# Contiguous 8 MB blocks and 64-byte result rows in a kernel that streams its input

## The chip, the cores and the metric

One core of one Trainium2 chip runs the kernel. The metric is the time of one execution on the device in microseconds (us). Ratios are the mean time of one kernel's runs over the mean of the kernel before's runs in the same rounds, so they are not quite the ratio of the medians that are quoted. Below 1 is faster than before.

Names used below: SP, ACT and DVE are the sync, scalar and vector engines. SP and ACT also issue DMAs; each has its own DMA queue (q1 for SP, q10 for ACT in the profile), and both queues are served by the same 16 DMA engines. SPq and ACTq are the instruction queues of SP and ACT. A packet is one record in the profile's list of DMA transfers: here one row of a load or store, moved by one engine. A DMA has landed when its completion semaphore says so. The pitch is the distance in memory between the starts of two neighbouring partitions' runs.

## The reference

```python
def setup_inputs():
    batch, seq, dim = 32, 512, 1024
    return {"x": np.random.randn(batch, seq, dim).astype(np.float32)}

def reference(x):
    return np.sum(np.maximum(x, 0), axis=-1).astype(np.float32)
```

That is 16384 rows of 1024 floats, 67.1 MB in and 64 KB out. Every input byte is read once.

## The kernel before

Each of the 128 partitions owns 128 consecutive rows (512 KB). A load takes 16 of a partition's rows, 64 KB in one run of addresses, so one load moves 8 MB in 128 runs that lie 512 KB apart. Seven such blocks are followed by smaller tiles of 8, 4, 2 and 1 rows, and the last row comes in four pieces, so that little work is left after the last byte. ACT sums the even rows of a tile and DVE the odd ones.

```python
xv = x_flat.rearrange("(p m) d -> p (m d)", p=P)                     # pitch 512 KB
out2d = out.rearrange("b s -> (b s)").rearrange("(p m) -> p m", p=P) # 504-byte rows in the store
big, tail, pieces = 16, [8, 4, 2, 1], [244, 252, 260, 268]
...
io_pool = ctx.enter_context(tc.tile_pool(name="io", bufs=2))
res = res_pool.tile([P, NT], fp32)
...
for j, cpd in enumerate(chunks):
    if cpd >= 8:   # the blocks and the 8-row tile share two buffers
        xt = io_pool.tile([P, cpd, D], fp32, tag="io", name=f"xt{j}")
    ...
    nc.sync.dma_start(out=xt, in_=xv[:, m0 * D : (m0 + cpd) * D]...)
    for c in range(cpd):
        m = m0 + c
        if m == NT - 2:
            act_op(xt[:, c, :], xt[:, c, :], m)
            nc.scalar.dma_start(out=out2d[:, 0 : NT - 2], in_=res[:, 0 : NT - 2])
        ...        # even rows act_op, odd rows dve_op
    m0 += cpd
...
for i, w in enumerate(pieces):       # the last row, in four pieces p0 .. p3
    ...
    nc.sync.dma_start(out=pt[:, 0:w], in_=xv[:, base + col : base + col + w])
    col += w
...                                  # DVE sums p0, p1, p2, then p3 with their sums
nc.sync.dma_start(out=out2d[:, NT - 2 : NT], in_=res[:, NT - 2 : NT])
```

There is one thing that the source doesn't show. The framework gives the DMAs eight completion semaphores in turn. A DMA that takes a semaphore for the second time must first wait until the DMA that used it before has landed. In the program as built, p3's load waits in this way on the load of the 8-row tile: the trace has eight such semaphores, 99, 100 and 103 to 108, and both of these loads carry 108.

## Time and profile before

| | before |
|---|---|
| median time | 164.37 us (3 runs, 164.32 to 164.52) |
| span in the trace | 162.7 us |
| load queue's share of the 16 DMA engines | 96.4% |
| DVE, ACT busy | 46%, 42% |
| 64 KB packets | 896, mean 2.441 us, most of them at 2.418 us |
| p3's load: issued, landed | 149.74 us, 159.77 us |
| DVE's last operation starts | 159.93 us |

The page of the kernel before, its busy times, its DMA queues and its chain of waits:

```profile
span 162.7 us, 347 instructions
DVE 74.3 (46%) x134; ACT 69.0 (42%) x129; POOL 0.2 (0%) x4
...
q1 hardware_dynamic: 2304, 67.11, 96.4%
q10 hardware_dynamic: 144, 0.06, 0.1%
...
DMA 78%; DVE 18%; SPq 1%; issue 0%; DVEq 0%
DMA xt<-in_x_dram 62%; DVE xt L49 17%; DMA p<-in_x_dram 17%; SPq L65 1%; DVE p L49 1%; DVEq L49 0%; DVEq L124 0%
```

The load queue (q1) takes 96.4% of what 16 engines have; no compute engine is busy for half of the span. The kernel is bound by its input. The packet records say the same more sharply: a packet of 64 KB takes 2.418 us, 27.1 GB/s on one engine, 434 GB/s on 16.

DVE's end in the kernel before, in order of time (start us, us, operation):

```profile
158.77 0.41 DVE L49 TENSOR_SCALAR_CACHE_REDUCE p<-p 128x244 f32<-128x244 f32 x1 [0.42 <-DMA p<-in_x_dram]
...
159.10 0.41 DVE L49 TENSOR_SCALAR_CACHE_REDUCE p<-p 128x252 f32<-128x252 f32 x1
...
159.46 0.42 DVE L49 TENSOR_SCALAR_CACHE_REDUCE p<-p 128x260 f32<-128x260 f32 x1
...
159.93 0.44 DVE L49 TENSOR_SCALAR_CACHE_REDUCE p<-p 128x271 f32<-128x271 f32 x1
```

The four pieces follow each other with no wait between them. That is what the pieces are for.

What SP's queue waited for in the kernel before (line, what ended the wait: us in total, times, longest):

```profile
SPq L65 <- DVE xt L49: 126.5, 6, 30.8
SPq L91 <- DMA xt<-in_x_dram: 16.4, 1, 16.4
SPq L98 <- DVE p L49: 10.3, 1, 10.3
...
```

The second line is p3's wait on the semaphore of the 8-row tile. It ends at 149.74 us, 8 us before p3's turn comes.

### The profile page before, as it was taken

Reading aid. Unit: us, or ns where it says so; the run is one execution under the profiler, and the core shown is the slowest. Engines: PE = TensorE matmul, PEld = TensorE weight load, DVE = VectorE, ACT = ScalarE, POOL = GpSimd, SP = SyncE. Lnnn points to the kernel's source line nnn. Section 1 sums busy time; section 2 is a strip of 40 time slices with the busy share of each in tenths; the row PEclk is TensorE's granted clock in tenths of the full one; section 3 lists DMA queues with packets and bytes.
Section 4 is the critical chain, followed back from the end, with each engine's and each line's share of the span. In section 5 each row is a group of like instructions: output and inputs, shape, how many; then the busy total and the mean of one; then the engine's idle time right before and its main releaser. Section 6 shows DMA issues by size and latency. Waiting matters only on the chain.

```text
span 162.7 us, 347 instructions
## 1 busy us (share of the span) xinstructions
DVE 74.3 (46%) x134; ACT 69.0 (42%) x129; POOL 0.2 (0%) x4
## 2 busy tenths in 40 slices
DVE  0000029900597007950099300992039900598983
ACT  3000029700595007930099100990039700596882
POOL 0000000000000000000000000000000000000000
DMA  7969969969969979979989998998997997999990
GB/s 258 483 290 516 499 274 516 499 274 516 500 274 516 516 306 467 516 338 435 516 356 421 499 403 387 516 419 354 516 467 306 516 467 306 451 443 395 405 362 23
DMA packets 2450, 67.19 MB, mean 413 GB/s; under 512 B 528, under 2 KB 1040, under 8 KB 1168
## 3 DMA queue, kind: packets, MB, share of 16 engines
q1 hardware_dynamic: 2304, 67.11, 96.4%
q10 hardware_dynamic: 144, 0.06, 0.1%
q14 instruction: 2, 0.02, 0.0%
HBM read 67.11 MB, written 0.07 MB: 413 GB/s over the span
## 4 chain that ended last, share of the span: by engine, by line
DMA 78%; DVE 18%; SPq 1%; issue 0%; DVEq 0%
DMA xt<-in_x_dram 62%; DVE xt L49 17%; DMA p<-in_x_dram 17%; SPq L65 1%; DVE p L49 1%; DVEq L49 0%; DVEq L124 0%
## 5 line engine op out<-in xcount | busy, mean ns | idle before, releaser
L49 DVE TENSOR_SCALAR_CACHE_REDUCE xt<-xt 128x1024 f32<-128x1024 f32 x63 | 72.6, 1215 | 85.7 <-DMA xt<-in_x_dram 85.4
L41 ACT ACTIVATE xt<-xt 128x1024 f32<-128x1024 f32 x64 | 66.7, 1043 | 90.3 <-DMA xt<-in_x_dram 90.3
L41 ACT ACTIVATION_READ_ACCUMULATOR xt<-xt 128x1 f32 x64 | 11.9, 186 | 0.0
L49 DVE DVE_READ_ACCUMULATOR xt<-xt 128x1 f32 x63 | 5.2, 83 | 0.0
L49 DVE TENSOR_SCALAR_CACHE_REDUCE p<-p 128x244 f32<-128x244 f32 (+3 forms) x4 | 1.6, 420 | 0.5 <-DMA p<-in_x_dram 0.4
L41 ACT ACT_TABLE_LOAD x1 | 1.3, 1283 | 0.7 <-PEq L113 0.7
L49 DVE DVE_READ_ACCUMULATOR p<-p 128x1 f32 x4 | 0.3, 83 | 0.0
L113 POOL MEMSET const-bfloat16-1.0<- 128x1 bf16 x1 | 0.1, 102 | 0.0
L113 POOL MEMSET const-uint8-127<- 128x1 uint8 x1 | 0.1, 101 | 0.0
L113 POOL MEMSET const-float32-0.0<- 128x1 f32 x1 | 0.1, 99 | 0.2 <-issue 0.2
L113 POOL MEMSET const-float32-1.0<- 128x1 f32 x1 | 0.1, 98 | 0.0
## 6 DMA issues: line engine op xcount, KB each, us to landing
xt<-in_x_dram SPq DMA_DIRECT2D x1, 4096.0 KB, 19.7
xt<-in_x_dram SPq DMA_DIRECT2D x1, 2048.0 KB, 24.2
xt<-in_x_dram SPq DMA_DIRECT2D x1, 1024.0 KB, 26.2
xt<-in_x_dram SPq DMA_DIRECT2D x1, 512.0 KB, 27.0
p<-in_x_dram SPq DMA_DIRECT2D x1, 134.0 KB, 10.0
p<-in_x_dram SPq DMA_DIRECT2D x1, 130.0 KB, 26.5
p<-in_x_dram SPq DMA_DIRECT2D x1, 126.0 KB, 26.7
p<-in_x_dram SPq DMA_DIRECT2D x1, 122.0 KB, 26.9
```

Of the source, the lines that this page charges most:

```text
L41: nc.scalar.activation(out=out_ap, in_=in_ap, func=mybir.ActivationFunctionType.Relu, accum_out=res[:, m : m + 1],)
L49: nc.vector.tensor_scalar(out=out_ap, in0=in_ap, scalar1=0.0, scalar2=None, op0=mybir.AluOpType.max, op1=mybir.AluOpType.add, accum_out=ac ...
L65: nc.sync.dma_start(out=xt, in_=xv[:, m0 * D : (m0 + cpd) * D].rearrange("p (c d) -> p c d", c=cpd),)
L113: nc = _bacc.Bacc("TRN2", target_bir_lowering=False, num_devices=1)
```

## The change

Its intent: each block of 8 MB becomes one contiguous stretch of memory (partition p takes 16 rows at p times 64 KB inside the block), in the hope that memory serves one stretch better than 128 runs that lie 512 KB apart. The price is on the output side. A partition's sums of one block are 16 floats, 64 bytes, and those of the next block go elsewhere, so the store of seven blocks has 128 x 7 rows of 64 bytes where it had 128 rows of 504 bytes. The sums now leave in three stores, and the 8-row tile has its own buffer.

```diff
-    xv = x_flat.rearrange("(p m) d -> p (m d)", p=P)
-    out2d = out.rearrange("b s -> (b s)").rearrange("(p m) -> p m", p=P)
+    xv = x_flat.rearrange("(j p c) d -> j p c d", j=NB, p=P)
+    ov = out.rearrange("b s -> (b s)").rearrange("(j p c) -> p j c", j=NB, p=P)
...
+    for j in range(NB - 1):
+        xt = io.tile([P, ROWS, D], fp32, tag="io", name=f"xt{j}")
+        nc.sync.dma_start(out=xt, in_=xv[j])
+        for c in range(ROWS):
+            row(xt[:, c, :], j, c)
+    nc.scalar.dma_start(out=ov[:, : NB - 1, :], in_=res[:, : NB - 1, :])
...
+    for n in TAIL:
+        xt = small.tile([P, n, D], fp32, name=f"t{n}")
+        nc.sync.dma_start(out=xt, in_=xv[j, :, c0 : c0 + n, :])
...
-                nc.scalar.dma_start(out=out2d[:, 0 : NT - 2], in_=res[:, 0 : NT - 2])
+                nc.scalar.dma_start(
+                    out=ov[:, j, : ROWS - 2], in_=res[:, j, : ROWS - 2]
+                )
...
-    nc.sync.dma_start(out=out2d[:, NT - 2 : NT], in_=res[:, NT - 2 : NT])
+    nc.sync.dma_start(out=ov[:, j, ROWS - 2 :], in_=res[:, j, ROWS - 2 :])
```

One more store shifts the turn of the semaphores by one: p3's load now waits on the middle store, the one of 896 rows.

More of the change, by code (lines that the diff above doesn't have):

```diff
@@ L6 @@
 from concourse._compat import with_exitstack
+ROWS = 16
+TAIL = [8, 4, 2, 1]
+PIECES = [244, 252, 260, 268]
 @with_exitstack
@@ L21, with row, dve @@
     N, D = x_flat.shape
-    assert N % P == 0
-    NT = N // P
-    xv = x_flat.rearrange("(p m) d -> p (m d)", p=P)
-    out2d = out.rearrange("b s -> (b s)").rearrange("(p m) -> p m", p=P)
-    big = 16
-    tail = [8, 4, 2, 1]
-    pieces = [244, 252, 260, 268]
-    assert sum(pieces) == D
-    nbig, rem = divmod(NT - sum(tail) - 1, big)
-    assert rem == 0
-    chunks = [big] * nbig + tail
-    io_pool = ctx.enter_context(tc.tile_pool(name="io", bufs=2))
-    res_pool = ctx.enter_context(tc.tile_pool(name="res", bufs=1))
-    res = res_pool.tile([P, NT], fp32)
-    def act_op(in_ap, out_ap, m):
-        nc.scalar.activation(
-            out=out_ap,
-            in_=in_ap,
-            func=mybir.ActivationFunctionType.Relu,
-            accum_out=res[:, m : m + 1],
-        )
-    def dve_op(in_ap, out_ap, accum_out):
+    NB = N // (P * ROWS)
+    assert N == NB * P * ROWS
+    assert sum(TAIL) == ROWS - 1 and sum(PIECES) == D
+    xv = x_flat.rearrange("(j p c) d -> j p c d", j=NB, p=P)
+    ov = out.rearrange("b s -> (b s)").rearrange("(j p c) -> p j c", j=NB, p=P)
+    io = ctx.enter_context(tc.tile_pool(name="io", bufs=2))
+    small = ctx.enter_context(tc.tile_pool(name="small", bufs=1))
+    res = small.tile([P, NB, ROWS], fp32)
+    def row(ap, j, c):
+        if c % 2 == 0:
+            nc.scalar.activation(
+                out=ap,
+                in_=ap,
+                func=mybir.ActivationFunctionType.Relu,
+                accum_out=res[:, j, c : c + 1],
+            )
+        else:
+            dve(ap, res[:, j, c : c + 1])
+    def dve(ap, accum_out):
         nc.vector.tensor_scalar(
-            out=out_ap,
-            in0=in_ap,
+            out=ap,
+            in0=ap,
             scalar1=0.0,
@@ L57, in dve_op @@
         )
-    m0 = 0
-    for j, cpd in enumerate(chunks):
-        if cpd >= 8:
-            xt = io_pool.tile([P, cpd, D], fp32, tag="io", name=f"xt{j}")
-        else:
-            xt = io_pool.tile([P, cpd, D], fp32, tag=f"t{cpd}", bufs=1, name=f"xt{j}")
-        nc.sync.dma_start(
-            out=xt,
-            in_=xv[:, m0 * D : (m0 + cpd) * D].rearrange("p (c d) -> p c d", c=cpd),
-        )
-        for c in range(cpd):
-            m = m0 + c
-            if m == NT - 2:
-                act_op(xt[:, c, :], xt[:, c, :], m)
-                nc.scalar.dma_start(out=out2d[:, 0 : NT - 2], in_=res[:, 0 : NT - 2])
-            elif (c % 2) == 0:
-                act_op(xt[:, c, :], xt[:, c, :], m)
-            else:
-                dve_op(xt[:, c, :], xt[:, c, :], res[:, m : m + 1])
-        m0 += cpd
@@ L80 @@
-    m_last = m0
-    assert m_last == NT - 1
-    base = m_last * D
-    np_ = len(pieces)
-    wlast = pieces[-1] + (np_ - 1)
-    ptiles = []
-    col = 0
-    for i, w in enumerate(pieces):
-        shape_w = w if i < np_ - 1 else wlast
-        pt = io_pool.tile([P, shape_w], fp32, tag=f"p{i}", bufs=1, name=f"p{i}")
-        ptiles.append(pt)
-        nc.sync.dma_start(out=pt[:, 0:w], in_=xv[:, base + col : base + col + w])
+    for j in range(NB - 1):
[3 more added lines that the diff above has]
+            row(xt[:, c, :], j, c)
@@ new lines @@
+    nc.scalar.dma_start(out=ov[:, : NB - 1, :], in_=res[:, : NB - 1, :])
+    j = NB - 1
+    c0 = 0
+    for n in TAIL:
+        xt = small.tile([P, n, D], fp32, name=f"t{n}")
+        nc.sync.dma_start(out=xt, in_=xv[j, :, c0 : c0 + n, :])
+        for c in range(n):
+            if c0 + c == ROWS - 2:
+                row(xt[:, c, :], j, c0 + c)
+                nc.scalar.dma_start(
+                    out=ov[:, j, : ROWS - 2], in_=res[:, j, : ROWS - 2]
+                )
+            else:
+                row(xt[:, c, :], j, c0 + c)
+        c0 += n
@@ L92 @@
+    np_ = len(PIECES)
+    parts = []
+    col = 0
+    for i, w in enumerate(PIECES):
+        extra = np_ - 1 if i == np_ - 1 else 0
+        pt = small.tile([P, w + extra], fp32, name=f"p{i}")
+        nc.sync.dma_start(out=pt[:, :w], in_=xv[j, :, ROWS - 1, col : col + w])
+        parts.append(pt)
         col += w
-    last = ptiles[-1]
+    last, w = parts[-1], PIECES[-1]
     for i in range(np_ - 1):
-        dve_op(ptiles[i], ptiles[i], last[:, pieces[-1] + i : pieces[-1] + i + 1])
-    dve_op(last, last, res[:, m_last : m_last + 1])
@@ L98 @@
-    nc.sync.dma_start(out=out2d[:, NT - 2 : NT], in_=res[:, NT - 2 : NT])
+        dve(parts[i], last[:, w + i : w + i + 1])
+    dve(last, res[:, j, ROWS - 1 : ROWS])
+    nc.sync.dma_start(out=ov[:, j, ROWS - 2 :], in_=res[:, j, ROWS - 2 :])
 _INS = ['x']
```

## The prediction

> **What bounds the kernel now.** The input stream. The page's queue part gives the load queue 96.4% of the 16 DMA engines' span; DVE is busy 46%, ACT 42%; the chain of waits is DMA 78%. In the trace's packet records each partition's 64 KB stretch is one packet; the 896 of them last 2.441 us on average and 2.418 us at the fastest, which is also typical (27.1 GB/s an engine, 434 GB/s for 16). Per engine 56 such packets are 135.4 us and the tail's smaller ones about 20 us: 155 of the 157.6 us between the first and the last load packet.
>
> **What the layout can give.** Little. The excess over 2.418 us is 0.023 us x 56 = 1.3 us an engine, 0.9 us of it in each engine's first four packets. [...] Nothing to remove: gain 0 to 1 us. Load packets and row instructions stay the same.
>
> **What it adds.**
> 1. A store of 128 x 7 rows of 64 B near the end: 56 packets an engine. Small stores in the trace take 9 ns (8 B) to 28 ns (504 B) a packet, about 20 ns with gaps: estimate 0.5 to 1.2 us of each engine, taken from the load stream: the store starts when block 6 is summed, about 149.4 us, with 10 us of loads queued.
> 2. A new wait. The built program makes the last piece's load (p3) wait on the semaphore of that store (before, on the 8-row tile's load, landed at 149.7 us). The skill (same page, Queues, rings and completion order) says that an engine goes round its queues by packet; no run here shows two busy queues. If one store packet goes between two load packets, 56 store packets need all of the about 50 load packets left, and the store lands near 159.5 us. Then p3 lands near 161.3 instead of 159.4, and the last DVE operation starts at about 161.4 instead of 159.93. That is critical: +1.5 to 2 us. If several store packets go per turn, the store lands by 155 us and the wait is free.
> 3. The store's issue sits on ACT before the last block: some 0.4 us, covered by ACT's idle time.
>
> **What it removes.** The 8-row tile has its own buffer, so the last 8 MB are requested at about 111 us instead of 130. The queue was never empty: worth nothing.
>
> **Prediction.** 165.8 us, 80% range 164.1 to 168.2. Faster by over 2%: 3%; within 2%: 83%; slower by over 2%: 14%.
>
> **What would show it.** 64 KB packets still at 2.418 us; the sync queue waiting 10 us or more at the last piece's line on the out store; DVE waiting 1 us or more for p before its last operation. Right about layout and wrong about the wait: p3 issued before 157 us and a time near 164.8.
>
> **What would make it wrong.** A cost of switching queues: two instruction fetches that fell between loads stretched the next load packet by 0.25 and 0.58 us. If each of 56 small packets did part of that: 168 to 175. Or the 64 KB pitch collides where 512 KB did not. Or the start's slow packets vanish and the wait doesn't bite: 163.5.

One sentence of the second paragraph is cut: it said that the Trainium skill has a pitch of 512 KiB halve a rate, which its page does not say (see the section on why the prediction was right or wrong). "Same page" in point 2 means DMA: Bandwidth & Descriptors.

## More of the kernel before

The DMAs issued in the last 15 us of the kernel before (tile, issuing queue, KB, us from issue to landing):

```profile
p<-in_x_dram SPq DMA_DIRECT2D x1, 134.0 KB, 10.0
out_dram<-res ACTq DMA_DIRECT2D x1, 63.0 KB, 1.6
out_dram<-res SPq DMA_DIRECT2D x1, 1.0 KB, 1.4
```

The first line is p3. Its 10.0 us are mostly time in the queue behind other loads, which costs nothing: its packets follow p2's directly. The large store lands in 1.6 us, after all loads.

## The result

| | before | changed |
|---|---|---|
| median time | 164.34 us (4 runs, 164.23 to 164.52) | 166.14 us (4 runs, 165.97 to 166.61) |
| ratio | 1 | 1.0117, 95% interval 1.0097 to 1.0136 |
| middle (large) store: issued, landed | 158.44, 160.05 us | 148.74, 158.99 us |
| p3's load: issued, landed | 149.74, 159.77 us | 159.01, 161.09 us |
| DVE's last operation starts | 159.93 us | 161.20 us |
| span | 162.7 us | 164.2 us |

The page of the changed kernel, the same lines:

```profile
span 164.2 us, 346 instructions
DVE 74.3 (45%) x134; ACT 69.0 (42%) x129; POOL 0.2 (0%) x4
...
q1 hardware_dynamic: 2304, 67.11, 95.3%
q10 hardware_dynamic: 1056, 0.06, 0.4%
...
DMA 75%; DVE 23%; issue 0%; DVEq 0%; SPq 0%; ACTq 0%
DMA xt<-in_x_dram 67%; DVE xt L50 22%; DMA out_dram<-res 6%; DMA p<-in_x_dram 1%; DVE p L50 0%; DVEq L50 0%; SPq L62 0%; ACTq L65 0%; DVEq L122 0%
```

The work of the engines is the same. New in the chain is the store, out_dram<-res, with 6% of the span: a store that nothing computes from stands on the way to the end.

The DMAs issued in the last 16 us of the changed kernel:

```profile
p<-in_x_dram SPq DMA_DIRECT2D x1, 134.0 KB, 2.1
out_dram<-res ACTq DMA_DIRECT2D x1, 56.0 KB, 10.3
out_dram<-res ACTq DMA_DIRECT2D x1, 7.0 KB, 2.0
out_dram<-res SPq DMA_DIRECT2D x1, 1.0 KB, 1.6
```

A store of 56 KB takes 10.3 us where 63 KB took 1.6 us. SP's waits in the changed kernel:

```profile
...
SPq L89 <- DMA xt<-in_x_dram: 26.1, 2, 19.0
SPq L89 <- DMA out_dram<-res: 19.3, 1, 19.3
...
```

The last line shown is p3's wait, now ended by the store. DVE's end in the changed kernel, the last two pieces:

```profile
158.84 0.42 DVE L50 TENSOR_SCALAR_CACHE_REDUCE p<-p 128x260 f32<-128x260 f32 x1
...
161.20 0.43 DVE L50 TENSOR_SCALAR_CACHE_REDUCE p<-p 128x271 f32<-128x271 f32 x1 [1.93 <-DMA p<-in_x_dram]
```

DVE stands 1.93 us idle for p3, and nothing is left to hide it.

Why the store takes 10.3 us can for the most part be counted in the packet records. Its first packet starts 3.7 us after the issue; before, the large store's first packet came 0.9 us after the issue. Wherever the first packet can be told apart, a store issued with several microseconds of loads queued waits 3.5 to 4.3 us for it; no run asked why. From the first packet (152.41 us) to its last (158.53 us), the 16 engines carry 896 store packets, 642 load packets and 96 four-byte packets that belong to the loads' completions. In the two microseconds from 153.0 to 155.0 us there are 103 store packets and 104 of the loads' packets. The counts are those of one store packet, then one load packet, whatever their sizes. The store packet itself takes 0.011 us; the load packet beside it takes 0.309 us or more at that time. Only when the loads run out, after 157.5 us, do the store packets go faster than that.

The Trainium skill (DMA: Bandwidth & Descriptors, section Queues, rings and completion order) says that an engine goes round its queues packet by packet, and that a packet typically holds some 9 to 17 descriptors. The turns are in this trace. The bunches are not: each 64-byte row is a packet of its own here.

### The profile page after: what moved, and what is told of

Same layout as the page of the kernel before. It is cut to its first block, busy times and chain, and to the rows that moved or that the text cites. A ratio compares the mean times of both kernels' runs of the same rounds, so it can differ in the third digit from the quotient of the medians.

```text
span 164.2 us, 346 instructions
## 1 busy us (share of the span) xinstructions
DVE 74.3 (45%) x134; ACT 69.0 (42%) x129; POOL 0.2 (0%) x4
## 3 DMA queue, kind: packets, MB, share of 16 engines
q1 hardware_dynamic: 2304, 67.11, 95.3%
## 4 chain that ended last, share of the span: by engine, by line
DMA 75%; DVE 23%; issue 0%; DVEq 0%; SPq 0%; ACTq 0%
DMA xt<-in_x_dram 67%; DVE xt L50 22%; DMA out_dram<-res 6%; DMA p<-in_x_dram 1%; DVE p L50 0%; DVEq L50 0%; SPq L62 0%; ACTq L65 0%; DVEq L122 0%
## 5 line engine op out<-in xcount | busy, mean ns | idle before, releaser
L50 DVE TENSOR_SCALAR_CACHE_REDUCE xt<-xt 128x1024 f32<-128x1024 f32 x56 | 64.4, 1215 | 84.2 <-DMA xt<-in_x_dram 84.2
L40 ACT ACTIVATE xt<-xt 128x1024 f32<-128x1024 f32 x56 | 58.3, 1043 | 86.9 <-DMA xt<-in_x_dram 86.9
L40 ACT ACTIVATION_READ_ACCUMULATOR xt<-xt 128x1 f32 x56 | 10.5, 188 | 0.0
L40 ACT ACTIVATE t<-t 128x1024 f32<-128x1024 f32 x8 | 8.4, 1048 | 2.7 <-DMA t<-in_x_dram 2.7
L50 DVE TENSOR_SCALAR_CACHE_REDUCE t<-t 128x1024 f32<-128x1024 f32 x7 | 8.2, 1216 | 0.8 <-DMA t<-in_x_dram 0.6
L50 DVE DVE_READ_ACCUMULATOR xt<-xt 128x1 f32 x56 | 4.6, 83 | 0.0
L40 ACT ACTIVATION_READ_ACCUMULATOR t<-t 128x1 f32 x8 | 1.5, 186 | 0.0
L50 DVE DVE_READ_ACCUMULATOR t<-t 128x1 f32 x7 | 0.6, 82 | 0.0
```

The lines of the kernel that those rows point to most:

```text
L40: nc.scalar.activation(out=ap, in_=ap, func=mybir.ActivationFunctionType.Relu, accum_out=res[:, j, c : c + 1],)
L50: nc.vector.tensor_scalar(out=ap, in0=ap, scalar1=0.0, scalar2=None, op0=mybir.AluOpType.max, op1=mybir.AluOpType.add, accum_out=accum_out,)
```

## The experiments

Theory W: the loss is the late issue of p3's load. It waits on the store's semaphore, and the store lands late because it has 56 packets an engine, which take turns with load packets. Rival S: 896 small packets cost the engines time that the loads then lack. Rival P: the new pitch loads slower. Rival B: the store's time goes by its bytes or by a fixed delay, not by turns.

| run | pitch of input | middle store | ratio to before (95%) |
|---|---|---|---|
| changed kernel | 64 KB | 896 packets of 64 B | 1.0117 (1.0097 to 1.0136) |
| e1, p3 waits on something else | 64 KB | 896 of 64 B | 1.0011 (0.9999 to 1.0023) |
| e2 | 512 KB | 896 of 64 B | 1.0159 (1.0144 to 1.0174) |
| e3 | 64 KB | 128 of 448 B | 0.9998 (0.9985 to 1.0011) |
| e4 | 512 KB | 128 of 448 B | 1.0008 (0.9996 to 1.0019) |
| e5, store in two, the first early | 64 KB | 512, then 384 of 64 B | 1.0093 (1.0078 to 1.0108) |
| e6, a store after each block | 64 KB | 7 times 128 of 64 B | 1.0013 (0.9999 to 1.0027) |
| e7, half rows | 64 KB | 2 times 896 of 32 B | 1.0171 (1.0146 to 1.0196) |
| e8, before again | 512 KB | as before | 1.0010 (0.9988 to 1.0032) |
| e9, before with the new pitch | 64 KB | as before | 1.0003 (0.9991 to 1.0016) |
| e10, before with p3 issued late | 512 KB | as before | 1.0124 (1.0108 to 1.0141) |

### e1: the wait taken away

```diff
-PIECES = [244, 252, 260, 268]
+PIECES = [496, 260, 268]
```

One DMA fewer before the last piece shifts its turn: it now waits on block 6's load. The store is untouched.

> The changed kernel with the first two pieces of the last row made one (496, 260, 268 columns): one DMA fewer, so the last piece's load no longer waits on the semaphore of the store of 64-byte rows, but on block 6's load (landed at 139.3 us). The store itself, its time of issue and its 896 packets stay. Theory W (the late wait of the last piece's load is the loss): the last piece lands within 0.5 us of the one before it, DVE's last operation starts before 159.9 us instead of 161.20, time about 164.5 us, ratio to before 0.998 to 1.003. Rival S (896 small packets take the engines' time from the loads): stays within 0.5 us of 166.1, ratio about 1.010. Rival P (the new pitch loads slower): also about 166.

Measured: 164.32 us (5 runs, 164.17 to 164.58), ratio 1.0011. The store still lands at 159.36 us. SP's queue and DVE's last operation in this run:

```profile
112.36 27.31 SPq L89 DMA_DIRECT2D p<-in_x_dram  x3
160.00 0.35 SPq L96 DMA_DIRECT2D out_dram<-res  x1
...
159.49 0.43 DVE L50 TENSOR_SCALAR_CACHE_REDUCE p<-p 128x270 f32<-128x270 f32 x1
```

All pieces are issued by 139.7 us, and DVE's last operation starts at 159.49 instead of 161.20 us. The 896 packets and the new pitch are both still there, so neither S nor P can hold the loss. The edit also spares DVE one small operation; e3 and e6 keep four pieces and agree.

### e2, e3, e4: pitch and store apart

```diff
 e2 and e4
-    xv = x_flat.rearrange("(j p c) d -> j p c d", j=NB, p=P)
+    xv = x_flat.rearrange("(p j c) d -> j p c d", j=NB, p=P)
 e3 and e4
-    ov = out.rearrange("b s -> (b s)").rearrange("(j p c) -> p j c", j=NB, p=P)
+    ov = out.rearrange("b s -> (b s)").rearrange("(p j c) -> p j c", j=NB, p=P)
```

In e2 and e3 the order of the rows is not the same on both sides, so the result is wrong; the work is the same. In e3 and e4 a partition's 112 sums are contiguous in the output, and the middle store has 128 rows of 448 bytes.

> The changed kernel with the input's old pitch of 512 KB, everything else as changed (rows are summed in the old order and stored in the new one, so the result is wrong on purpose; times are not touched by that). Theory W: as slow as the changed kernel plus what the new pitch gave, 0.3 to 0.8 us: about 166.7 us, ratio 1.011 to 1.018. Rival P: back to about 164.4. Rival S: about 166.5, as W.

> The changed kernel with its new input pitch, but the sums laid out so that the middle store has 128 rows of 448 bytes (8 packets an engine, not 56; result wrong on purpose). The last piece's load still waits on that store. Theory W with packets taken in turns: 8 store packets need about 8 load packets, the store lands before 156 us, the last piece is issued in time, time about 163.9 us, ratio 0.994 to 1.000. Rival S: also about 164. Rival P: about 166. If the store lands after 158 all the same (a cost of the store that does not go by its packets), about 166.

> Old pitch, rows of 448 bytes, right result: of the change only the three stores and the own buffer of the 8-row tile remain. Theory W: about 164.4 us, ratio 0.998 to 1.003; the last piece is issued before 157 us. The difference to the run with the new pitch and 448-byte rows is the pitch alone: expected 0.3 to 0.8 us, the new pitch faster, seen in the 64 KB packets of the first four blocks (mean 2.44 against 2.42 us). If the pitch does nothing and the profile of before was one odd draw: no difference.

Measured: e2 166.81 us, e3 164.08 us, e4 164.26 us. With either pitch the kernel is slow with 64-byte rows and at par with 448-byte rows, although p3's load waits on the same semaphore in all three. The DMAs of the last 20 us in e3, p3 and the middle store:

```profile
p<-in_x_dram SPq DMA_DIRECT2D x1, 134.0 KB, 3.3
out_dram<-res ACTq DMA_DIRECT2D x1, 56.0 KB, 7.2
```

The store of the same 56 KB with 8 packets an engine, issued at 148.98 us, lands at 156.14 us; p3 is issued at 156.16 us, while loads are still queued before it, and DVE's last operation starts at 159.58 us. SP's wait on the store and DVE's last operation in e3:

```profile
SPq L89 <- DMA out_dram<-res: 16.2, 1, 16.2
...
159.58 0.43 DVE L50 TENSOR_SCALAR_CACHE_REDUCE p<-p 128x271 f32<-128x271 f32 x1
```

So the wait is not wrong in itself; it must end before the loads run out. Here it ended 2.4 us before the last packet of the piece p2 (158.60 us), and that was early enough; 158.30 us, in e5 below, was too late. No run lies between. e4, which keeps the three stores and the own buffer of the 8-row tile, is at par too, so these are not the loss.

e2 over the changed kernel would give the old pitch a loss of 0.4% (1.0159 against 1.0117); e4 over e3 gives 0.1% (0.2 us), less than the 0.3 to 0.8 us expected. Some 0.5 us of e2's excess is p3's load, which took 2.56 us to land where the changed kernel's took 2.08. e9 below settles the pitch nearer zero.

### e5: a store issued 60 us before it is needed

```diff
+        if j == 3:
+            nc.scalar.dma_start(out=ov[:, :4, :], in_=res[:, :4, :])
-    nc.scalar.dma_start(out=ov[:, : NB - 1, :], in_=res[:, : NB - 1, :])
+    nc.scalar.dma_start(out=ov[:, 4 : NB - 1, :], in_=res[:, 4 : NB - 1, :])
```

> The changed kernel with its middle store cut in two: blocks 0 to 3 (512 rows of 64 bytes, 32 packets an engine) leave as soon as block 3 is summed, at about 90.5 us, while loads of 64 KB packets have the engines; blocks 4 to 6 (24 packets an engine) where the store was. Theory T (an engine takes one store packet after one load packet, whatever their sizes): the early store, 33 KB, needs 32 load packets: about 16 of 64 KB, 8 of 32 KB, 8 of 16 KB, and so lands only at 150 to 154 us, some 60 us after its issue; the second store lands at 157.5 to 158.5; the last piece is late by 0 to 0.7 us; time 164.0 to 165.0. Rival B (store packets are taken in bunches, or the store takes a time that goes by its bytes or by a fixed delay): the early store lands within 15 us, by 106 us, the second by 156 us, and the time is about 164.1.

Measured: 165.73 us (4 runs, 165.50 to 165.81), ratio 1.0093. The DMAs of e5, its first two stores and p3:

```profile
p<-in_x_dram SPq DMA_DIRECT2D x1, 134.0 KB, 2.6
...
out_dram<-res ACTq DMA_DIRECT2D x1, 32.0 KB, 60.2
out_dram<-res ACTq DMA_DIRECT2D x1, 24.0 KB, 9.2
```

The early store, 32 KB, takes 60.2 us: issued at 90.35, landed at 150.58 us. From its first packet to 139 us the engines carry 350 of its packets and 350 of the loads' packets, completions included. In 16 of the first 18 stretches of 2.42 us exactly 16 store packets start, one for each engine; in the other two it is 32, where the packets of a load's completion give 16 more turns. That is theory T in that expectation, and it rules out B: beside packets of 2.418 us a row of 64 bytes costs one whole turn. The time missed its range (164.0 to 165.0): the second store landed at 158.29 us as expected, but p3, issued then, took 2.57 us to land and not the 2.1 us of the changed kernel, which is 0.5 of the 0.7 us above the range. Issuing the store earlier helps little as long as 24 packets an engine remain for the tail.

### e6: a store after each block

```diff
         for c in range(ROWS):
             row(xt[:, c, :], j, c)
-    nc.scalar.dma_start(out=ov[:, : NB - 1, :], in_=res[:, : NB - 1, :])
+        nc.scalar.dma_start(out=ov[:, j, :], in_=res[:, j, :])
```

> The changed kernel with right results, but each block's sums leave when the block is summed: seven stores of 128 rows of 64 bytes, 8 packets an engine each. Only the last of them is in flight in the tail, and 8 packets need 8 load packets. Theory W with turns: it lands near 156 us, the last piece's load (which waits on an earlier DMA) is not late: time 163.9 to 164.3, ratio 0.997 to 1.001, 1.8 us better than the change and at par with before or a little better. Rival S (the 896 small packets cost the engines time wherever they stand): 164.8 or more.

Measured: 164.34 us (6 runs, 164.15 to 164.67), ratio 1.0013, just above the range; result right. The same 896 packets of 64 bytes, spread over the run, leave at most 0.3% between this kernel and before (the end of the interval); S is out as the cause of the loss. Of the seven stores the first five take 22.1 to 24.4 us each (8 turns with 64 KB packets are 19.3 of them), the sixth 16.7 and the last 7.2 us. It lands at 156.03 us, and p3, whose load turned out to wait on it here too, is issued at 156.04 us, in time. This repairs the change; it does not beat the kernel before, and no other version run does.

### e7: twice the packets, the same bytes

```diff
-    nc.scalar.dma_start(out=ov[:, : NB - 1, :], in_=res[:, : NB - 1, :])
+    for h in (0, ROWS // 2):
+        nc.scalar.dma_start(
+            out=ov[:, : NB - 1, h : h + ROWS // 2],
+            in_=res[:, : NB - 1, h : h + ROWS // 2],
+        )
```

> The changed kernel with its middle store as two of half rows: 1792 packets of 32 bytes, 112 an engine, same bytes; the last piece's load waits on the second of them. Theory W with turns: the load packets run out at 158.5 us with over half of the store packets left, which then go at about 20 ns each: the second store lands at 160.0 to 160.8, the last piece's load is issued then, DVE's last operation starts about 1.2 us later than in the changed kernel (161.20): near 162.5 us, time 167.0 to 167.8. Rival B (time by bytes): 166.1, as the changed kernel.

Measured: 166.89 us (4 runs, 166.59 to 167.54), ratio 1.0171, just under the range. DVE's last operation starts at 162.32 us, as expected, but by another road in part. The first half store needs only the first eight sums of a block and left at 144.12 us, 4.6 us sooner than I had thought, so the second landed at 159.40 us and not after 160. The rest is p3's load, which took 2.79 us this time. More packets cost more at equal bytes, against B, but of the 1.12 us by which DVE's last operation is later than in the changed kernel, only 0.41 is the later landing of the store; 0.71 is p3's load. As a measure of the dose this run is blurred.

### e8: the kernel before, once more

> The kernel before, unchanged, as a control for what a second trace of it shows. The ratio should be 1.000 within 0.002. If the old pitch slows the early blocks' 64 KB packets, the packets of the blocks 0 to 3 average 2.43 us or more again (first trace: 2.637, 2.442, 2.434, 2.447, 2.419, 2.423, 2.422, 2.425 us in groups of 64) against 2.418 to 2.421 from the second group on in the three runs with the new pitch; if that was one odd draw, they are near 2.419 too.

Measured: 164.18 us (4 runs, 164.00 to 164.96), ratio 1.0010. The old pitch's early packets are uneven again: 2.591, 2.459, 2.486 and 2.444 us in the first four groups of 64, then 2.420 and 2.480 us. So the trace of before was no odd draw, but the cost is small and changes from run to run.

### e9: the new pitch alone

The kernel before with its loads from the contiguous blocks and its stores as they were (wrong result):

```diff
+    xb = x_flat.rearrange("(j p c) d -> j p c d", p=P, c=16)
-            in_=xv[:, m0 * D : (m0 + cpd) * D].rearrange("p (c d) -> p c d", c=cpd),
+            in_=xb[m0 // 16, :, m0 % 16 : m0 % 16 + cpd, :],
-        nc.sync.dma_start(out=pt[:, 0:w], in_=xv[:, base + col : base + col + w])
+        nc.sync.dma_start(out=pt[:, 0:w], in_=xb[NT // 16 - 1, :, 15, col : col + w])
```

> The kernel before with the input's new pitch of 64 KB alone, its two stores left as they are (rows are summed in the new order and stored in the old one: wrong on purpose, times untouched). The pitch by itself: the mean 64 KB packet falls from 2.435 to 2.446 us (four traces with the old pitch) to 2.431 to 2.434 us (five with the new), which is 0.1 to 0.8 us over an engine's 56; time 163.4 to 164.1, ratio 0.996 to 1.000. Rival P (new pitch slower): above 1.002.

Measured: 164.09 us against 164.05 us, ratio 1.0003 (0.9991 to 1.0016), a hair above the range and clear of rival P's 1.002. The mean packet was 2.438 us this time, inside the span of the old pitch; e10, with the old pitch, has 2.428 us, below all that were seen with the new one. The intent of the change is worth nothing that five rounds can see.

### e10: the wait alone

The kernel before, right result, no packet and no instruction more. DVE's sum of p0 writes its rectified values (which nobody reads) into p3's buffer, so p3's load has to wait for that operation:

```diff
     for i, w in enumerate(pieces):
         ...
+        if i == np_ - 1:
+            dve_op(ptiles[0], pt[:, 0 : pieces[0]], pt[:, w : w + 1])
         nc.sync.dma_start(out=pt[:, 0:w], in_=xv[:, base + col : base + col + w])
...
-    for i in range(np_ - 1):
+    for i in range(1, np_ - 1):
```

> The kernel before, result right, with no packet and no instruction added: DVE's sum of the first piece writes its rectified values into the last piece's buffer, so the last piece's load cannot be issued before that operation is done, about 159.2 us, in place of 149.7 us. Theory W (the late issue of the last piece's load is enough by itself): the load lands 2.1 to 2.6 us after its issue, at 161.3 to 161.9, DVE's last operation starts 1.4 to 2.0 us after the 159.93 of before; time 165.5 to 166.3, ratio 1.008 to 1.013, as the change. If the small packets were needed for the loss: at most 0.5 us slower than before.

Measured: 166.15 us (4 runs, 165.84 to 166.18), ratio 1.0124. The wait of SP that is new, and DVE's last operation:

```profile
SPq L93 <- DVE p L49: 9.8, 1, 9.8
```

```profile
161.61 0.43 DVE L49 TENSOR_SCALAR_CACHE_REDUCE p<-p 128x271 f32<-128x271 f32 x1 [2.09 <-DMA p<-in_x_dram]
```

p3's load is issued at 158.85 us and lands at 161.50 us. The late issue of one load of 134 KB makes the whole difference of the change by itself, with the old pitch, the old stores and no small packets. e1 shows that the wait is needed for the loss, e10 that it is enough.

## Why the prediction was right or wrong

- **The bound: right.** The 64 KB packets stay at 2.418 us in most cases, and the load queue's share fell from 96.4% to 95.3% only because the end became longer.
- **The layout gives 0 to 1 us: right, at its lower end.** e9 finds 0.03% with an interval of about 0.13% each way. The prediction misread the Trainium skill here. For copies between HBM tensors, DMA: Bandwidth & Descriptors, section Latency and other measured facts, gives 207 GB/s at a row pitch of 512 KiB and calls 214 GB/s full; it has about half only at 4 MiB and 8 MiB. The misreading did no harm, because the prediction followed the trace. Loads into SBUF show no clear loss at 512 KB either: the mean 64 KB packet took 2.428 to 2.446 us in five traces with the old pitch and 2.431 to 2.438 us in seven with the new one.
- **The new wait: right, step by step.** The store was to land near 159.5 us and landed at 158.99; p3 near 161.3 and 161.09; DVE's last operation at 161.4 and 161.20; SP's wait of 10 us or more on the store was 19.3 us. Of the two ways of taking turns, the first held: one store packet to one load packet. The store's first packet came some 3 us later than the prediction had it (152.41 us, not about 149.4), so the loads ran out before the store did; its last packets then went faster and it landed on time all the same.
- **The small packets' own time, 0.5 to 1.2 us: too large.** They took 0.011 us each, 56 of them 0.6 us of an engine, and e6, which has them all and no late wait, is 0.13% (0.2 us) from before, with an interval that reaches to nothing. The wait was worth what was put down: e10 measures 2.0 us (1.24% of 164.05 us), at the top of the 1.5 to 2 us that were predicted.
- **The number: in part luck.** Added to 164.37 us, the middles of the prediction's own terms (less 0.5 for the layout, 0.85 for the packets, 1.75 for the wait) give 166.5 us. It put 165.8 and does not say why it went lower. That this came close to 166.14 us tells less than the steps of the wait do, which the runs confirm one by one.
- **The dangers named: absent.** Small packets between large ones did not hold up the loads in a way that shows (e1, e6), and the new pitch collides with nothing (e9).

What stays open is why p3's load, issued when the other loads have run out, took 2.08 to 2.79 us to land (in the changed kernel, e2, e5, e7 and e10), where a store of 63 KB took 1.6 us. In all five its first packet starts 0.9 to 1.0 us after the issue, and it lands 0.3 us after the end of its last packet. In between, some of its 1072-byte packets were slow: the slowest took 0.25 to 1.1 us, by run, in place of 0.048 us; no run asked why.

## What to carry to other kernels

In these runs a store that shared its engines with a bulk stream took turns with it packet by packet. After the first 3.5 to 4.3 us, its time was about the number of its packets on one engine times the packet time of the stream, as long as the stream lasted: count the rows of a store, not its bytes, and spread a store of many short rows over the run. After any change in the number of DMAs, look at which earlier DMA each late load now waits for: a semaphore that comes round again can tie the last load of a stream to a slow store that it has nothing to do with. To prove such a wait, take it away in the slow kernel and put it alone into the fast one.

## What the Trainium skill lacked or had wrong

- DMA: Bandwidth & Descriptors, Queues, rings and completion order: it puts typically 9 to 17 descriptors into one turn of a queue. Stores issued from ACT took turns with loads from SP row by row: 350 store packets to 350 load packets in e5, where 32 KB in 64-byte rows took 60.2 us.
- No page was found that has row pitches for loads from HBM into SBUF. Loads of 64 KB runs at a pitch of 512 KB ran at 27.1 GB/s an engine (2.418 us a packet), and a pitch of 64 KB changed the time by 0.03%.
- No page was found that tells why the same load, issued when the stream has run out, can take so unequal a time: 134 KB took 2.08 to 2.79 us from issue to landing.
- No page was found that tells how long a store waits for its first packet beside queued loads: 3.5 to 4.3 us here, against 0.9 us for a store issued when less than 1 us of loads was left.
